# More sevenfold weight pairs in the down projection of a hybrid decoder layer, with more of their sums made ahead

## The chip, the cores and the metric

The kernel runs on one core of a Trainium2 chip. The metric is the device time of one execution in microseconds, the median of several. Less is better. The core has five engines with queues of their own: TensorE (PE; its weight loads are listed as PEld), VectorE (DVE), ScalarE (ACT), GpSimd (POOL) and SyncE (SP). SP, ACT and POOL also issue DMA transfers.

## The reference

One decoder layer over 256 tokens of width 2048, in float32. It is cut here to the order of its products; the change touches the last line alone, and the place of some vector work beside the others.

```python
h = rmsnorm(x, norm_mix_pre)
xr, yr, q, k, v, g_rnn, g_attn = split(h @ w_in)
y_rnn = rg_lru(conv(xr)) * gelu(yr)
y_att = sliding_window_sink_attention(rope(q), rope(k), v)
mix = sigmoid(g_rnn) * (y_rnn @ w_rnn_proj) + sigmoid(g_attn) * (y_att @ w_attn_proj)
x = x + rmsnorm(mix @ w_out, norm_mix_post)
u = square(relu(rmsnorm(x, norm_mlp_pre) @ w_mlp_up))      # 2048 -> 8192
return x + rmsnorm(u @ w_mlp_down, norm_mlp_post)          # 8192 -> 2048
```

## The kernel before

**Products in three parts.** Every float32 matrix is split into a high part (a cast, `Stream.two`, L176, on ACT) and a low part (source minus high, `Stream.low`, L181, on DVE). A product of two matrices is three matmuls: high by high, high by low, low by high (`product`, L1255). Weights stream through the class `Stream` in chunks of 128 x 2048 numbers (1 MB), each cut into items of 128 x 1024: a load on SP's queue into a raw slot, a cast on ACT into a `whi` slot, a subtraction on DVE into a `wlo` slot, then matmuls on PE. There are 4 raw slots and 6 high and low slots (L37), plus slots that a stage adds where it has room (`Stream.add`). `half` hands out one item of a plain chunk; before each, `ahead` emits the splits and loads of as many later items as there are slots.

**Stages.** Attention and gates projections, the recurrent branch, the attention and recurrent projections, the merge, the output projection (`o_pass`), and then the MLP in two halves `f` = 0, 1 of 4096 inner channels. A half has an up stage (16 calls of `a_pair` or `up_pair`, one per pair `p` of 256 inner channels, each 4 items) and two down passes `n` = 0, 1 (`down`, L1268 ff.), one per half of the output columns. A down pass works through the same 16 pairs.

**Plain and sevenfold pairs.** A plain pair in a down pass is 2 items by 4 output quarters: 8 products, 24 matmuls of 128 x 512. A sevenfold pair (`Stream.seven`, `LEFT`) forms sums of quarters of the weights (T1 to T4) and of the activations, as in Strassen's scheme in Winograd's form, and needs 7 products, 21 matmuls. It has 3 items of 128 x 1024 and one more piece of 128 x 512 (`t2`), which has 2 raw, 2 high and 2 low slots of its own. The products of a sevenfold pair go to seven PSUM banks: P1 and P6 in one `pair` tile, Q5 and N7 in the other, and P2, Q3, Q4. The first two tiles have the tag that the up stage's `ps` also uses (two buffers). Plain pairs use P2, Q3, Q4 and Cs. The products of one sevenfold pair are sorted by the weight they need: P1, Q3, P2, Q4, N7, Q5, P6.

**Who makes the sums.** `KINDS[f][n]` (L41) has one letter per pair. "1" is plain. For "3" DVE makes all sums as the pair is split (L149 to L151: one addition of 1024 columns and two of 512). For "4" all were made long before and lie in DRAM, so the pair loads 1.75 MB. For "2" T1 and T2 lie in DRAM (1.25 MB are loaded) and one subtraction on DVE (L147, 1024 columns) gives the third item; it needs `t2`, loaded by L114, and the first item.

**Sums ahead.** `sums_ahead` (L405 ff.) is a generator: a 1 MB load into an `early` buffer on POOL's queue (L410), four steps later two or one additions of 512 columns on DVE, a step later two more, then a store of 1 MB (kind 4) or 0.5 MB (kind 2) on POOL's queue (L422). `in_turn(n, every, wait)` starts n of them, one every `every` steps, after `wait` steps; a step is one call of `half` or `seven`. The buffers come from the pool `big` (12 units of 8 KB a partition), which also holds activations.

**Order.** Loops are unrolled. The tile framework lists the instructions of each engine at compile time in an order of its own within the dependences, and puts in the waits; the splits of sevenfold pairs are tied to program order on DVE and ACT (`behind_latest`). Each engine then works through its list in order, DMA issues on SP too. A buffer that is used again is waited for: the load of `t2` of a pair waits for the last reader of the `t2` two sevenfold pairs back, which is its low part (L181, `t2lo`).

At the end of an up stage the last `ps` tile is read by a copy on ACT (L359) and an addition on DVE (L360).

Of the kernel before, what the change touches and what calls it, by code (L numbers as in the profile page):

```python
# [18 lines left out]
F32 = mybir.dt.float32  # L19
F32R = mybir.dt.float32r  # L20
# [5 lines left out]
P = 128  # L26
# [11 lines left out]

PAIRS = 16

KINDS = ("1243414242143211", "1243414242143211"), ("1243441243424111", "1243441243424111")  # L41
SEVENS = [[p for p in range(PAIRS) if k[0][p] != "1"] for k in KINDS]


# [197 lines left out]
def layer(tc, x, few, kx_first, kx_rest, pos_row, gains, w_q, w_xy, w_rg, w_g, w_rp, w_ap, w_out,  # L242
# [44 lines left out]
    def unit(name, dt=F32R):  # L287
        return big.tile([P, 4, 2, S], dt, tag="U8", name=name)

    def flat(t):  # L290
        return t.rearrange("p a b c -> p (a b c)")
# [3 lines left out]
    def units(name):  # L295
        return [unit(f"{name}{i}") for i in range(4)]
# [507 lines left out]


    m1 = []
    ws.side.append(in_turn(11, 4, 16))
    for g in range(NKV):
        m1.append(pa.tile([P, TB, 512], F32, tag="m1", bufs=4, name=f"m1{g}"))
        for tb, b in enumerate(b_pass512(hT, two_banks("g"), 1)):  # L810
# [131 lines left out]
    for m in range(4):  # L942
        recur(m)
        if m == 0:
            pump(99)
            ctx_ps.close()
            psg = ctx1.enter_context(tc.tile_pool(name="psg", bufs=2, space=bass.MemoryType.PSUM))
            pairs.append(ctx1.enter_context(tc.tile_pool(name="psa2", bufs=1, space=bass.MemoryType.PSUM)))
        if m < 2:
            ws.side.append(in_turn(2, 6))  # L950
            for i in range(2):
                attn_proj(2 * m + i)
        if m < 3:
            gates(m)
# [83 lines left out]

    r1 = []
    late = []  # L1040
    h2T = units("h2T")

    def square(tb, q, b):
# [224 lines left out]
    def down(f, n, uT, held, order, finish, early, between=lambda p: None, behind=lambda: None, closing=False):  # L1268
# [8 lines left out]
        def step(p, i, hi, lo, name, at=0, w=512, into=None):  # L1277
            tb, n2 = name
            b = into or PLACE[name]
            o = 0 if into else at  # L1280
            t = slice(tb * P, tb * P + P)
            c = slice(n2 * 512 + at, n2 * 512 + at + w)
            a = uT[p][:, i]
            product(banks[b][:, o : o + w], (a[:, 0, t], a[:, 1, t]), (hi[:, c], lo[:, c]), b in begun,
                    p == PAIRS - 1 and i == 1, w < 512 and not into)
            begun.add(b)

        ready = {}
        for p in range(PAIRS - held - closing):
            if p in SEVENS[f]:  # L1290
# [3 lines left out]
                for name in names:  # L1294
                    i, w = LEFT[name]
                    product(banks[name], left(uT[p], i), parts[w], name in begun,
                            p == SEVENS[f][-1] and (name in ("P1", "P6", "Q5", "N7") or closing and name == PLACE[order[-1]]))
                    begun.add(name)
                if p == SEVENS[f][-1]:
                    for name in ((1, 0), (0, 0), (1, 1), (0, 1)):  # L1300
# [46 lines left out]
    for f in range(2):  # L1347
        uT = {}
        rooms = []
        if f:  # L1350
            ws.side.append(in_turn(7, 7))
        full = []
        for p in range(PAIRS):
            u = u2("u")
            if f == 0 and p == 1:
                ws.side.append(in_turn(6, 6, 16))
            if f == 0 and p in (4, 6):
                not_before(nc.gpsimd.dma_start(h2T_away[p // 2 - 2], h2T[p // 2].bitcast(F32)))
            if f == 0 and p < 2:
# [4 lines left out]
            if f == 0 and p == R2_AT:  # L1364
                pump(99)
                ctx3.close()
                pc = ctx2.enter_context(tc.tile_pool(name="pc", bufs=1))
                ws.small = pc
                ws.t2_raws, ws.t2_highs, ws.t2_lows = [[Slot() for i in range(2)] for k in range(3)]
                ws.add(ws.raws, pc.tile([P, 1024], F32, name="xraw"))  # L1370
            if f == 1 or p >= R2_AT:
                for q, u in full:
                    if q % 2 == 0:
# [7 lines left out]
                    evacuate(f, q, u, uT[q])  # L1381
                full.clear()
        order = [(1, 1), (1, 0), (0, 0), (0, 1)]
        more = [flat(unit("more", dt)) for dt in (F32, F32R)]
        for slots, room in ((ws.raws, more[0]), (ws.raws, more[0]), (ws.highs, more[1]), (ws.lows, more[1])):
            at = len(ws.added) % 2
            ws.add(slots, room[:, at * 1024 : at * 1024 + 1024])
        if f == 0:
            for n in range(2):
                def finish(name, b, t, *part):  # L1390
# [170 lines left out]
```

## Time and profile before

| | us |
|---|---|
| median of 3 runs | 1484.26 |
| lowest, highest | 1483.44, 1484.67 |
| the profiled execution | 1485.31 |
| its span, first to last instruction | 1483.5 |
| PE busy | 1473.4 |
| DVE busy | 1163.0 |
| ACT busy | 878.4 |

All times inside the kernel are from the profiled execution, from its span's start. Matmuls are pipelined, so a matmul's own duration is longer than its share of PE's time: what one costs is the distance from its start to that of the next. The same holds for DVE, where an instruction may begin a little before the one ahead of it has ended.

### The profile page before, as it was taken

How to read it: one execution, taken by the hardware profiler on the slowest of the kernel's cores; microseconds unless marked ns; L12 is line 12 of the kernel's file. 1: busy time of each engine (PE TensorE's matmuls, PEld its weight loads, DVE VectorE, ACT ScalarE, POOL GpSimd, SP SyncE). 2: the span in 40 equal slices, each digit the busy share in tenths (PEclk: the TensorE clock that was granted, in tenths of full speed). 3: DMA queues.
4: the chain of work that ended last, by engine and by line, in shares of the span. 5: the costliest groups of instructions: out<-in, count | busy, mean ns of one | idle time of the engine just before them, and what ended most of it. 6: DMA issues, size and time to landing. Idle time of an engine off the chain costs nothing.

```text
span 1483.5 us, 20572 instructions
## 1 busy us (share of the span) xinstructions
PE 1473.4 (99%) x7532; PEld 1250.5 (84%) x7532; DVE 1163.0 (78%) x1509; ACT 878.4 (59%) x1246; POOL 41.3 (3%) x83
## 2 busy tenths in 40 slices
PE   9999999999999999999999999999999999999997
PEld 8887788888889888888889888888888888888886
DVE  6687888869679967666757868788897777789997
ACT  8564565647566766444345756576565555666573
POOL 0000000000000000000000000000000000000000
PEclk9999999999999999999999999999999999999999
DMA  9778875585856567987764898888898778679795
GB/s 340 234 248 329 293 281 178 195 289 170 279 184 220 171 199 256 322 328 266 288 203 140 294 335 289 284 271 297 281 338 321 279 276 289 233 237 334 263 321 206
DMA packets 109830, 391.68 MB, mean 264 GB/s; under 512 B 12192, under 2 KB 12448, under 8 KB 101024
## 3 DMA queue, kind: packets, MB, share of 16 engines
q1 hardware_dynamic: 96192, 314.85, 61.5%
q0 software_dynamic: 10656, 70.26, 13.2%
q10 hardware_dynamic: 2880, 5.24, 0.9%
q8 instruction: 59, 0.97, 0.3%
q14 instruction: 43, 0.35, 0.1%
HBM read 351.51 MB, written 38.80 MB: 263 GB/s over the span
## 4 chain that ended last, share of the span: by engine, by line
PE 95%; DVE 3%; DMA 1%; ACT 1%; issue 0%; DVEq 0%; ACTq 0%
PE ps L332 22%; PE ps L330 11%; PE s L1255 8%; PE dQ L1255 8%; PE pp L372 4%; PE pp L370 4%; PE pp L374 4%; PE dP L1255 4%; PE g L370 4%; PE g L374 4%; PE g L372 4%; PE dCs L1255 2%; PE o L370 2%; PE o L372 2%; PE o L374 2%; PE q L370 2%
## 5 line engine op out<-in xcount | busy, mean ns | idle before, releaser
L181 DVE TENSOR_TENSOR wlo<-wraw,whi 128x1024 fp32r<-128x1024 f32 x444 | 539.0, 1221 | 209.0 <-ACT whi L176 204.7
L176 ACT CAST whi<-wraw 128x1024 fp32r<-128x1024 f32 x440 | 459.8, 1051 | 387.3 <-PE ps L332 89.7
L332 PE MATMUL ps<-h2T,whi 128*128 128x512 f32 x704 | 170.8, 391 | 0.3 <-DVE st L487 0.3
L332 PEld LDWEIGHTS ps<-h2T,whi 128*128 128x128 f32 x704 | 130.3, 188 | 26.2 <-DVE st L487 0.5
L332 PE MATMUL ps<-hT,whi 128*128 128x512 f32 x512 | 120.6, 391 | 0.0
L332 PEld LDWEIGHTS ps<-hT,whi 128*128 128x128 f32 x512 | 94.8, 188 | 19.4 <-issue 0.7
L370 PE MATMUL g<-whi,hT 128*128 128x512 f32 x256 | 100.9, 394 | 0.0
L372 PE MATMUL g<-wlo,hT 128*128 128x512 f32 x256 | 99.9, 390 | 0.0
L374 PE MATMUL g<-whi,hT 128*128 128x512 f32 x256 | 99.8, 390 | 0.0
L330 PE MATMUL ps<-h2T,wlo 128*128 128x256 f32 x704 | 91.8, 283 | 0.0
L330 PEld LDWEIGHTS ps<-h2T,wlo 128*128 128x128 f32 x704 | 89.6, 192 | 2.3
L1255 PE MATMUL dQ<-whi,uT 128*128 128x512 f32 (+1 forms) x210 | 78.2, 384 | 0.0
L176 ACT CAST whi<-more 128x1024 fp32r<-128x1024 f32 x48 | 50.2, 1053 | 35.3 <-DMA acc_away<-t 8.0
L181 DVE TENSOR_TENSOR wlo<-more,whi 128x1024 fp32r<-128x1024 f32 x48 | 58.1, 1222 | 10.8 <-ACT whi L176 9.6
L330 PEld LDWEIGHTS ps<-hT,wlo 128*128 128x128 f32 x512 | 63.7, 192 | 2.1 <-issue 0.8
L330 PE MATMUL ps<-hT,wlo 128*128 128x256 f32 x512 | 64.7, 284 | 0.0
L181 DVE TENSOR_TENSOR wlo<-xraw,whi 128x1024 fp32r<-128x1024 f32 x47 | 57.4, 1221 | 8.7 <-ACT whi L176 8.4
L176 ACT CAST whi<-xraw 128x1024 fp32r<-128x1024 f32 x47 | 49.2, 1048 | 20.2 <-PE ps L332 13.7
L370 PEld LDWEIGHTS g<-whi,hT 128*128 128x128 f32 x256 | 48.1, 188 | 10.5 <-issue 1.0
L1255 PE MATMUL s<-whi,uT 128*128 128x512 f32 (+1 forms) x166 | 56.5, 383 | 0.0
L374 PEld LDWEIGHTS g<-whi,hT 128*128 128x128 f32 x256 | 48.1, 188 | 10.0
L372 PEld LDWEIGHTS g<-wlo,hT 128*128 128x128 f32 x256 | 48.1, 188 | 9.5
(345 smaller groups left out, 2992.3 us busy)
## 6 DMA issues: line engine op xcount, KB each, us to landing
wraw<-in_w_up SPq DMA_DIRECT2D x103, 512.0 KB, 5.3
early<-in_w_dn POOLq DMA_DIRECT2D x36, 1024.0 KB, 8.4
wraw<-in_w_g SPq DMA_DIRECT2D x64, 512.0 KB, 5.2
wraw<-in_w_xy SPq DMA_DIRECT2D x64, 512.0 KB, 4.0
wraw<-in_w_dn SPq DMA_DIRECT2D x55, 512.0 KB, 5.9
away<-early POOLq DMA_DIRECT2D x22, 1024.0 KB, 6.6
wraw<-in_w_q SPq DMA_DIRECT2D x32, 512.0 KB, 5.4
wraw<-in_w_ap SPq DMA_DIRECT2D x32, 512.0 KB, 4.5
```

The lines of the kernel that those rows point to most:

```text
L176: self.pin(self.nc.scalar.copy(hi, src))
L181: self.latest_low = self.pin(self.nc.vector.tensor_tensor(lo, src, hi.bitcast(F32), ALU.subtract))
L330: mm(ps[:, f, 1, :], w, a[:, 0, :], start=False, stop=j == 1 and k == 7)
L332: mm(ps[:, f].rearrange("p a b -> p (a b)"), w, a.rearrange("p a b -> p (a b)"), start=kt == 0, stop=j == 3 and k == 7)
L370: mm(banks[tb][n], a[:, 0, t], hi[:, n * 512 : n * 512 + 512], start=first, stop=False)
L372: mm(banks[tb][n], a[:, 0, t], lo[:, n * 512 : n * 512 + 512], start=False, stop=False)
L374: mm(banks[tb][n], a[:, 1, t], hi[:, n * 512 : n * 512 + 512], start=False, stop=last)
L1255: mm(b, a[x], w[y], start=not begun and i == 0, stop=tail and i == 2, skip_group_check=shared)
```

## The change

14 instead of 11 pairs of each pass of the first half are sevenfold, and 12 instead of 11 in the second; the letters are dealt anew, so that kind "3" occurs 2 times instead of 8, "2" 24 instead of 14 and "4" 26 instead of 22. The sums made ahead rise from 36 chunks to 50: 13 instead of 11 in the attention stage (starting after 10 steps instead of 16), 3 instead of 2 in each attention projection, 8 as before in the merge, 4 new ones in the output projection, 9 every 4 steps instead of 6 every 6 in the first up stage, and 10 every 5 instead of 7 every 7 in the second. The first pair of every down pass, plain before, is sevenfold. There are now 14 `three` buffers instead of 11; for that the raw slot `xraw` is gone, and the second half's down passes get two raw slots more from a third `more` unit. So raw slots are 4 instead of 5 in the up stages, 6 instead of 7 in the first half's down passes, and 8 instead of 7 in the second's. The remaining lines set a matmul's `stop` flag where the last product now is.

```diff
--- before.py
+++ after.py
@@ -38,7 +38,7 @@
 
 PAIRS = 16
 
-KINDS = ("1243414242143211", "1243414242143211"), ("1243441243424111", "1243441243424111")
+KINDS = ("4242424242424211", "4242242242242411"), ("4242434242421111", "4242434242441111")
 SEVENS = [[p for p in range(PAIRS) if k[0][p] != "1"] for k in KINDS]
 
 
@@ -804,7 +804,7 @@
 
 
     m1 = []
-    ws.side.append(in_turn(11, 4, 16))
+    ws.side.append(in_turn(13, 4, 10))
     for g in range(NKV):
         m1.append(pa.tile([P, TB, 512], F32, tag="m1", bufs=4, name=f"m1{g}"))
         for tb, b in enumerate(b_pass512(hT, two_banks("g"), 1)):
@@ -947,7 +947,7 @@
             psg = ctx1.enter_context(tc.tile_pool(name="psg", bufs=2, space=bass.MemoryType.PSUM))
             pairs.append(ctx1.enter_context(tc.tile_pool(name="psa2", bufs=1, space=bass.MemoryType.PSUM)))
         if m < 2:
-            ws.side.append(in_turn(2, 6))
+            ws.side.append(in_turn(3, 7))
             for i in range(2):
                 attn_proj(2 * m + i)
         if m < 3:
@@ -1038,6 +1038,7 @@
 
     r1 = []
     late = []
+    ws.side.append(in_turn(4, 6, 2))
     h2T = units("h2T")
 
     def square(tb, q, b):
@@ -1282,7 +1283,8 @@
             c = slice(n2 * 512 + at, n2 * 512 + at + w)
             a = uT[p][:, i]
             product(banks[b][:, o : o + w], (a[:, 0, t], a[:, 1, t]), (hi[:, c], lo[:, c]), b in begun,
-                    p == PAIRS - 1 and i == 1, w < 512 and not into)
+                    (p == PAIRS - 1 or closing and p == PAIRS - held - 2 and name == order[-1]) and i == 1,
+                    w < 512 and not into)
             begun.add(b)
 
         ready = {}
@@ -1294,7 +1296,8 @@
                 for name in names:
                     i, w = LEFT[name]
                     product(banks[name], left(uT[p], i), parts[w], name in begun,
-                            p == SEVENS[f][-1] and (name in ("P1", "P6", "Q5", "N7") or closing and name == PLACE[order[-1]]))
+                            p == SEVENS[f][-1] and name in ("P1", "P6", "Q5", "N7")
+                            or closing and p == PAIRS - held - 2 and name == PLACE[order[-1]])
                     begun.add(name)
                 if p == SEVENS[f][-1]:
                     for name in ((1, 0), (0, 0), (1, 1), (0, 1)):
@@ -1348,12 +1351,12 @@
         uT = {}
         rooms = []
         if f:
-            ws.side.append(in_turn(7, 7))
+            ws.side.append(in_turn(10, 5))
         full = []
         for p in range(PAIRS):
             u = u2("u")
             if f == 0 and p == 1:
-                ws.side.append(in_turn(6, 6, 16))
+                ws.side.append(in_turn(9, 4, 8))
             if f == 0 and p in (4, 6):
                 not_before(nc.gpsimd.dma_start(h2T_away[p // 2 - 2], h2T[p // 2].bitcast(F32)))
             if f == 0 and p < 2:
@@ -1366,8 +1369,7 @@
                 ctx3.close()
                 pc = ctx2.enter_context(tc.tile_pool(name="pc", bufs=1))
                 ws.small = pc
-                ws.t2_raws, ws.t2_highs, ws.t2_lows = [[Slot() for i in range(2)] for k in range(3)]
-                ws.add(ws.raws, pc.tile([P, 1024], F32, name="xraw"))
+                ws.t2_raws, ws.t2_highs, ws.t2_lows = [[Slot() for i in range(n)] for n in (2, 2, 2)]
             if f == 1 or p >= R2_AT:
                 for q, u in full:
                     if q % 2 == 0:
@@ -1381,10 +1383,9 @@
                     evacuate(f, q, u, uT[q])
                 full.clear()
         order = [(1, 1), (1, 0), (0, 0), (0, 1)]
-        more = [flat(unit("more", dt)) for dt in (F32, F32R)]
-        for slots, room in ((ws.raws, more[0]), (ws.raws, more[0]), (ws.highs, more[1]), (ws.lows, more[1])):
-            at = len(ws.added) % 2
-            ws.add(slots, room[:, at * 1024 : at * 1024 + 1024])
+        more = [flat(unit("more", dt)) for dt in (F32, F32R) + f * (F32,)]
+        for i, slots in enumerate((ws.raws, ws.raws, ws.highs, ws.lows) + f * (ws.raws, ws.raws)):
+            ws.add(slots, more[i // 2][:, i % 2 * 1024 : i % 2 * 1024 + 1024])
         if f == 0:
             for n in range(2):
                 def finish(name, b, t, *part):
```

## Rows read from the trace of the kernel before

**Rows 1.** The page, part 1: the span, and busy time of each engine.

```profile
span 1483.5 us, 20572 instructions
PE 1473.4 (99%) x7532; PEld 1250.5 (84%) x7532; DVE 1163.0 (78%) x1509; ACT 878.4 (59%) x1246; POOL 41.3 (3%) x83
```

**Rows 2.** The chain that ended last, in order of time: start, us, instructions; first half's first down pass.

```profile
1016.60 2.72 PE s L1255 x12
```

**Rows 3.** Stretches: us, busy time (instructions) of five engines, clock, DMA share, GB/s.

```profile
842.41:975.77 133.36, 133.36 (x770) 118.16 (x769) 101.98 (x135) 80.13 (x107) 7.50 (x14) 1.00 0.83 293
979.04:1058.60 79.56, 79.56 (x353) 65.92 (x351) 71.08 (x73) 51.38 (x58) 0.00 (x0) 1.00 0.86 292
1058.60:1138.20 79.60, 79.60 (x353) 65.96 (x352) 70.89 (x72) 50.19 (x56) 0.00 (x0) 1.00 0.90 320
1315.97:1395.50 79.53, 79.53 (x352) 65.93 (x351) 73.57 (x78) 52.57 (x64) 0.00 (x0) 1.00 0.90 313
...
1125.00:1132.00 7.00, 7.00 (x32) 5.82 (x31) 6.39 (x8) 2.72 (x4) 0.00 (x0) 1.00 1.02 392
```

**Rows 4.** DVE in order of time (start, us, line, operation), last down pass.

```profile
1410.32 1.22 DVE L181 TENSOR_TENSOR more<-wraw,more 128x1024 fp32r<-128x1024 f32 x1
...
1413.72 0.69 DVE L181 TENSOR_TENSOR t2lo<-t,t2hi 128x512 fp32r<-128x512 f32 x1
1414.32 1.22 DVE L181 TENSOR_TENSOR wlo<-xraw,whi 128x1024 fp32r<-128x1024 f32 x1
...
1437.01 0.68 DVE L181 TENSOR_TENSOR t2lo<-t,t2hi 128x512 fp32r<-128x512 f32 x1
...
1441.62 1.22 DVE L147 TENSOR_TENSOR wraw<-t,more 128x1024 f32<-128x1024 f32 x1
...
1446.16 0.68 DVE L181 TENSOR_TENSOR t2lo<-t,t2hi 128x512 fp32r<-128x512 f32 x1
1446.76 1.22 DVE L181 TENSOR_TENSOR wlo<-wraw,whi 128x1024 fp32r<-128x1024 f32 x1
```

**Rows 5.** DVE in order of time, the first half's first down pass.

```profile
1008.71 0.69 DVE L181 TENSOR_TENSOR t2lo<-t,t2hi 128x512 fp32r<-128x512 f32 x1
...
1015.23 1.22 DVE L147 TENSOR_TENSOR wraw<-t,more 128x1024 f32<-128x1024 f32 x1
```

**Rows 6.** SP's DMA issues in order of time: two loads of `t2`.

```profile
1009.42 0.33 SPq L114 DMA_DIRECT2D t<-away  x1
...
1437.72 0.32 SPq L114 DMA_DIRECT2D t<-away  x1
```

**Rows 7.** Line L114 over the span, all loads of `t2` of kind 2.

```profile
L114 SPq DMA_DIRECT2D t<-away x14: 320/326/425, 837.2 to 1437.7; - x14
...
DMA to landing us min/median/max: 3.0/5.2/7.0
```

**Rows 8.** Line L119 over the span: the first item's loads of sevenfold pairs.

```profile
DMA to landing us min/median/max: 3.3/6.3/8.3
```

**Rows 9.** All engines in order of time, where each up stage ends (PE, then DVE).

```profile
979.04 0.39 PE L1255 MATMUL dQ<-whi,uT 128*128 128x512 f32 x1
...
981.39 0.69 DVE L360 TENSOR_TENSOR u<-ps,u 128x512 f32<-128x512 f32 x1
...
1315.97 0.39 PE L1255 MATMUL dQ<-whi,uT 128*128 128x512 f32 x1
...
1318.33 0.69 DVE L360 TENSOR_TENSOR u<-ps,u 128x512 f32<-128x512 f32 x1
```

**Rows 10.** The page, parts 2 and 6: GB/s by fortieths; DMA issues, KB, us to landing.

```profile
GB/s 340 234 248 329 293 281 178 195 289 170 279 184 220 171 199 256 322 328 266 288 203 140 294 335 289 284 271 297 281 338 321 279 276 289 233 237 334 263 321 206
...
wraw<-in_w_up SPq DMA_DIRECT2D x103, 512.0 KB, 5.3
early<-in_w_dn POOLq DMA_DIRECT2D x36, 1024.0 KB, 8.4
...
away<-early POOLq DMA_DIRECT2D x22, 1024.0 KB, 6.6
```

## The prediction

> **What bounds the kernel now.** I read the page first. PE is busy for 1473.4 of 1483.5 us, DVE for 1163.0, ACT for 878.4 [rows 1]. A busy PE need not be PE at its rate, so the next view is the chain that ended last: inside a down pass it is PE alone, 12 matmuls of 128 x 512 in 2.72 us [rows 2], 0.2267 us each. A plain pair (24) then costs 5.44 us, a sevenfold one (21) 4.76. A pass of 11 sevenfold and 5 plain pairs should take 11 x 4.76 + 5 x 5.44 = 79.56 us. The table by stretches has the passes at 79.56, 79.60 and 79.53, with the clock at 1.00 throughout [rows 3]. So PE never waits there, and the passes are bound by the count of matmuls. The same table shows what is near: DVE is busy for 71.1, 70.9 and 73.6 us of these passes, and the DMA engines for 0.86 to 0.90 of them. The reader is to see a kernel with one bound and two others close under it: a saving on PE counts in full only as far as DVE and DMA keep up.
>
> **What the change removes.** 3 + 3 pairs in the first half's passes and 1 + 1 in the second's turn sevenfold: 8 pairs, 8 x 3 = 24 matmuls, 24 x 0.2267 = 5.44 us. All lie on PE's unbroken chain, so all count, if nothing new makes PE wait. The passes would go to 77.52 us (first half) and 78.88 (second).
>
> **What it puts on DVE.** A low part begins 1.13 us after the one before it and a `t2lo` takes 0.60: a kind 4 pair goes from start to the next start in 1410.32 to 1414.32, 4.00 us; a kind 2 pair, with its subtraction, in 1441.62 to 1446.76, 5.14 us [rows 4]. PE gives a sevenfold pair 4.76. Kinds 4 and 2 in turn average 4.57, so DVE keeps up on average, at 96%; the first pass has seven of each, 64.0 us against 66.6 for PE. In the second pass eight are kind 2: 65.1 against 66.6. The plain pairs, which let DVE catch up (4 low parts would be 2.27 us of 5.44 for each), are gone from the middle of these passes. The dearer kind 3 is nearly gone too, which is why the sum holds. Activations of the 8 extra pairs and the 14 extra chunks summed ahead cost DVE some 1 to 2.4 us each (two to four additions or casts' low parts of 0.60) in stages where it is busy for 102 of 133 us [rows 3]; I cost them at nothing there, since a low part that is late by one such group is covered by six `whi` slots, each worth more than 2.7 us of PE.
>
> **The wait that decides: `t2`.** A kind 2 pair begins on DVE with a subtraction that needs its `t2`, and that load waits for the `t2lo` two sevenfold pairs back (two slots). With a kind 4 pair between, DVE has 4.00 us of work to cover the load. Two cases in the trace show it. After the `t2lo` that ended at 1437.69 the load went out at 1437.72 and the subtraction began at 1441.62, with no idle time, 3.93 us later [rows 4, 6]. After the one that ended at 1009.40 the load went out at 1009.42 and the subtraction began at 1015.23, 5.83 us later, 1.8 more than the pair between takes [rows 5, 6]. All 14 such loads took 3.0 to 7.0 us, median 5.2 [rows 7]. With L for that latency and 0.1 us for the release, two pairs (4, 2) cost DVE 5.14 + L + 0.1 as soon as L exceeds 3.9, and PE 9.52: they keep pace up to L = 4.3. Above it DVE falls back by L - 4.3 every two pairs and eats its lead.
>
> The first pass worked through, from its start: I take pair 1's `t2lo` done at 2.6 us (the slots full as now, one more low part, `t2lo` and the addition L360), pair 2 at 7.8 with one more activation, pair 3 at 12.95. Pairs 5, 7, 9, 11, 13 follow at 5.24 + L each. PE needs pair 13's first item at 13 x 4.76 = 61.88; it is there 2.87 us (two low parts and `t2lo`) before that pair's end. At L = 5.0 this is 12.95 + 51.2 - 2.87 = 61.3, in time by 0.6. At L = 5.6 it is 64.3, and PE stands for 2.4 us. In the second pass the letters go 4, 2, 2, so there is one wait in three pairs, and the same count gives 0 at 5.0 and 1.7 at 5.6. The second half gives 0 and 0.4, and for the last pass, with its extra scalings on DVE, 0.5 and 1.8. I take L = 5.0, the middle of 3.0 to 7.0 and a little under the median: 0.5 us in all. The ends are 0 (L up to 4.4) and, at L = 7.0 throughout, over 20 us; that nobody sees for six loads in a row here.
>
> **The raw slots.** With six in the first half's passes, a pair's first load goes out when the first low part two pairs back is done; from 9.52 us some 2.3 go for its own low part and cast, which leaves 7.2 us. These loads took 6.3 us in the median and 8.3 at most [rows 8]. Nothing at the median, 1 us now and then at the worst; it acts in the same direction as a long L and belongs to that rival.
>
> **A cover that goes.** The first pair of a pass is now sevenfold. In the first pass of each half its fifth product, N7, goes to the pair tile that the up stage's last `ps` occupied, and that is read by L360. PE's first matmul is at 979.04, L360 ends at 982.08; in the second half 1315.97 and 1319.02 [rows 9]. Before, a plain pair that uses other banks hid this for 5.44 us. Now N7 is wanted 4 x 0.68 = 2.72 us after the start, and is free after 3.04 to 3.05: 0.33 us and a release, say 0.4, twice: 0.8 us. If L360 is listed one low part later it is 1.5 each, if earlier nothing.
>
> **Sums ahead, and DMA.** Extra loads and stores ride on POOL's queue, on which nothing else waits but the two stores of h2T. Most new ones lie in stages with room: the output projection, and the earliest steps of attention (fortieths of 140 to 250 GB/s near them, [rows 10]). The tight place is the first up stage, one sum per pair instead of one per 1.5. A pair there takes 133.36 / 12 = 11.11 us [rows 3] and loads 4 x 0.524 MB, 189 GB/s; a sum reads 1.05 MB and writes 1.05 or 0.52 (five of nine are kind 4), 168 GB/s; the stores of h2T, 2.1 MB over some 100 us, 21. Together 377 GB/s, against 293 at a DMA share of 0.83 now. While loads were bunched the engines moved 392 GB/s at a share of 1.02 [rows 3]. So it fits, without room to spare, and I cost it at nothing: cover is the lead of six items. The Trainium skill speaks against it: DMA: Bandwidth & Descriptors, Specifications, gives one core about 358 GB/s of HBM. By that the 100 us would take 5 us longer and the change would come out at 1484 or 1485, no change. The row of 392 is above that figure; it is 7 us, not 100.
>
> **Sum.** -5.44 + 0.8 + 0.5 = -4.1 us. The profiled execution took 1485.31, 1.05 above the median of 1484.26, which is in the spread of the runs; I set the sum against the median: **1480.1 us**. Against the profiled execution itself it would be 1481.2.
>
> **Rivals.** (1) The `t2` chain runs out of lead. With the DMA engines fuller L goes to 5.6: stalls of 2.4 + 1.7 + 0.4 + 1.8 = 6.3 us, so 1484.26 - 5.44 + 0.8 + 6.3 = 1485.9. For it: the median of 5.2 is already over 4.3, and the first half's passes will move more (1.75 and 1.25 MB a pair in turn, one raw slot less). Against it: the last pass had 3.93 us without a wait, and a DVE that is behind issues its loads later, into emptier queues. (2) Slower: the first up stage is bound by DMA. By proportion of the share, 293 / 0.83 = 353 GB/s is the limit, and no fortieth of the span held over 341 [rows 10]. At 341, 100 us of 377 GB/s take 10.6 us longer; when the six items of lead are spent PE waits in the up stage or enters the pass without lead: 1484.26 - 4.64 + 10.6 = 1490.2. Below about 352 GB/s sustained the change ends over 0.2% slower. Against: 392 in the bunched stretch. (3) The passes don't lose 24 matmuls, or the saved time was hidden: the even 0.2267 us and the sums of 79.56 speak against, 2 in 100.
>
> **How the numbers follow.** Forecast 0.50; rival 1 0.30; rival 2 0.18; rival 3 0.02. A measurement of this kernel tells some 0.2%, 3.0 us, from no change. Faster by more (under 1481.3) is the forecast, 0.50. Within it lie rival 1, except its worst, and rival 3: 0.31. Slower (over 1487.2) takes rival 2 and the worst of rival 1: 0.19. The low end is the full 5.44 us with no stall, 1478.8, less 0.3 of spread; the high end goes to 1489, most of the way into rival 2.
>
> **What would show it.** Right: 7508 matmuls; first-half passes of 77.5 and second-half ones of 78.9 us; a PE gap of 0.3 to 0.5 us ahead of N7 at each first pass; subtractions on L147 that wait for `t2` on DMA in nearly every kind 2 pair without PE waiting. Rival 1: gaps on PE ahead of a product with `whi`, `wlo` or `t2lo`, growing late in the passes. Rival 2: pairs of the first up stage longer than 11.11 us, with low parts waiting for casts and casts for loads, at 340 to 355 GB/s. Wrong altogether: stalls in the attention or projection stages, where new `early` buffers could push out others of the 12.

## The result and the profile after

The changed kernel is slower. It takes 1496.63 us (median of 5, 1489.85 to 1499.53), the kernel before beside it 1484.67 (1483.44 to 1485.38): ratio 1.0077, 95% interval 1.0064 to 1.0090. 1480.1 was predicted, and the measured time lies above every one that the prediction gave, its worst rival (1490.2) included. Its executions lie further apart than those of before, over some 10 us, and the profiled one was the fastest: 1489.85 us, span 1488.0. A second profile, of the same kernel in the first experiment, took 1498.65. Both are needed to see the loss.

The page, part 1, answers [rows 1]: 24 matmuls are gone, and PE's busy time fell by 0.8 us, where 5.44 were due.

```profile
span 1488.0 us, 20759 instructions
PE 1472.6 (99%) x7508; PEld 1243.7 (84%) x7508; DVE 1199.6 (81%) x1579; ACT 890.3 (60%) x1266; POOL 56.3 (4%) x111
```

The table of stretches answers [rows 3]: us, busy time (instructions) of PE, its weight loads, DVE, ACT and POOL, clock, DMA share, GB/s. The rows are twelve pairs of the first up stage and the first half's two down passes.

```profile
844.10:977.50 133.40, 133.40 (x770) 118.15 (x769) 109.02 (x153) 82.04 (x110) 10.13 (x19) 1.00 0.90 335
980.75:1058.66 77.91, 77.83 (x344) 64.11 (x342) 72.85 (x74) 54.08 (x64) 0.00 (x0) 1.00 0.92 318
1058.66:1140.93 82.27, 79.70 (x343) 63.57 (x342) 75.27 (x77) 55.02 (x62) 0.00 (x0) 1.00 0.93 325
```

The up stage is as long as before (133.36), with DMA at 335 GB/s. The first pass takes 77.91 us, 0.4 over the 77.52 of its matmuls; the second takes 82.27, 4.75 over, longer than the 79.60 it took with three sevenfold pairs less. (In the second profile they lose 2.3 and 5.8.) So the wait that PE never had in a down pass is there now.

Set beside before, matmul by matmul, the time goes as follows (us; in brackets the stall above the matmuls' own time, 155.0 for the first half's two passes, and 158.1 for the second's with the 0.34 of smaller matmuls at the very end):

| | before | after | after, second profile |
|---|---|---|---|
| lost up to the first down pass | 0 | 1.7 | 5.5 |
| first half's two passes | 159.1 | 160.2 (5.1) | 163.1 (8.1) |
| second half's two passes | 159.5 | 161.2 (3.1) | 163.3 (5.2) |

The first line is the start of the first down pass against the one in the profile of before; other kernels here, with no gap at the gates, came there up to 1.7 us sooner, so it is good to a microsecond or two. In it 1.7 us in both profiles fall to the gates, near 480 us; the second profile loses 3.8 more ahead of and in the output projection. That makes three places. The experiments take them in turn.

### The profile page after: what moved, and what is told of

It is laid out like the page before. It is cut to its first block, busy times and chain, and to the rows that moved or that the text cites. A ratio compares the mean times of both kernels' runs of the same rounds, so it can differ in the third digit from the quotient of the medians.

```text
span 1488.0 us, 20759 instructions
## 1 busy us (share of the span) xinstructions
PE 1472.6 (99%) x7508; PEld 1243.7 (84%) x7508; DVE 1199.6 (81%) x1579; ACT 890.3 (60%) x1266; POOL 56.3 (4%) x111
## 3 DMA queue, kind: packets, MB, share of 16 engines
q10 hardware_dynamic: 2880, 5.24, 0.9%
## 4 chain that ended last, share of the span: by engine, by line
PE 75%; DVE 10%; DMA 9%; ACT 3%; issue 3%; SPq 0%; DVEq 0%; ACTq 0%
PE ps L332 19%; PE ps L330 10%; DVE wlo L181 5%; PE pp L374 4%; PE pp L372 4%; PE pp L370 4%; PE g L370 4%; PE g L374 4%; PE g L372 4%; DMA more<-in_w_dn 3%; PE dQ L1256 3%; PE s L1256 2%; PE q L370 2%; PE q L374 2%; PE q L372 2%
## 5 line engine op out<-in xcount | busy, mean ns | idle before, releaser
L176 ACT CAST whi<-wraw 128x1024 fp32r<-128x1024 f32 x481 | 502.0, 1050 | 427.7 <-PE pp L374 71.1
L181 DVE TENSOR_TENSOR wlo<-wraw,whi 128x1024 fp32r<-128x1024 f32 x485 | 587.1, 1222 | 167.8 <-ACT whi L176 166.5
L372 PE MATMUL g<-wlo,hT 128*128 128x512 f32 x256 | 99.7, 389 | 0.0
L176 ACT CAST whi<-more 128x1024 fp32r<-128x1024 f32 x61 | 63.4, 1050 | 28.4 <-DMA more<-in_w_dn 12.7
L181 DVE TENSOR_TENSOR wlo<-more,whi 128x1024 fp32r<-128x1024 f32 x61 | 73.4, 1221 | 2.8 <-ACT whi L176 2.0
L1256 PE MATMUL s<-whi,uT 128*128 128x512 f32 (+1 forms) x190 | 64.8, 384 | 0.0
L1256 PE MATMUL dQ<-whi,uT 128*128 128x512 f32 (+1 forms) x172 | 62.5, 384 | 0.0
L370 PEld LDWEIGHTS g<-whi,hT 128*128 128x128 f32 x256 | 48.1, 188 | 10.5 <-issue 1.0
L410 POOL DMA_DIRECT2D early<-in_w_dn x50 | 26.8, 536 | 793.4 <-DVE wlo L181 500.8
L372 PEld LDWEIGHTS g<-wlo,hT 128*128 128x128 f32 x256 | 48.1, 188 | 9.5
L414 DVE TENSOR_TENSOR early<-early 128x512 f32<-128x512 f32 x50 | 34.4, 688 | 25.5 <-DMA early<-in_w_dn 25.2
```

What stands on the lines that cost most here:

```text
L176: self.pin(self.nc.scalar.copy(hi, src))
L181: self.latest_low = self.pin(self.nc.vector.tensor_tensor(lo, src, hi.bitcast(F32), ALU.subtract))
L370: mm(banks[tb][n], a[:, 0, t], hi[:, n * 512 : n * 512 + 512], start=first, stop=False)
L372: mm(banks[tb][n], a[:, 0, t], lo[:, n * 512 : n * 512 + 512], start=False, stop=False)
L410: not_before(nc.gpsimd.dma_start(w, chunks[c]))
L414: v.tensor_tensor(t1, t1, t3, ALU.add)
```

## Experiments: the parts that cost little, and the sums ahead

**The change again, unedited.** 

> The changed kernel once more, unedited, for a profile of another execution: the one on hand took 1489.85 us and four others 1496.0 to 1499.5, so some 7 us of the loss are in no trace yet. Theory A, the loops of slots in the down passes (a load waits for the split that frees its slot, the split for the load): all of the extra time lies in the four down passes, which took 160.2 us for the first half's two and 161.0 for the second's and would be 5 to 10 us longer together, and the up stages stay at 11.11 us a pair. Theory B, the DMA engines are overfull in the first up stage (339 GB/s there): that stage, 146.8 us from 833.0 on, is 3 to 8 us longer instead. Theory C, early buffers that keep others out: the extra time is before 800 us, around the gates, where this trace already loses 1.7 us.

1495.32 us, ratio 1.0064 (1.0044 to 1.0084). The loss repeats; the third column of the table is its profile.

**The raw slots alone**: before, with the slots of after.

```diff
-                ws.add(ws.raws, pc.tile([P, 1024], F32, name="xraw"))
...
+        more = [flat(unit("more", dt)) for dt in (F32, F32R) + f * (F32,)]
...
```

> The kernel before with one part of the change, the raw slots: no xraw, two more in the second half's down passes; letters and sums ahead as before. Theory A in its form for the raw slots: passes with plain pairs between have time to spare, so little is lost, 1484 to 1487 us, but loads wait for slots more often in the first half's passes. Theory B: no change in what is moved, 1484.3. If four raw slots in the up stages are what hurts, a pair there is over 11.11 us and the time 1487 to 1495.

1485.18 us, 1.0003 (0.9994 to 1.0013): no change that the times can tell. The profile does show one: PE waits once, at 992 us, for a low part, and the first half's passes take 160.5 us where before they took 159.1. So with the letters of before six raw slots cost some 1.3 us there, in this one profile.

**The output projection's sums alone**, added to before.

```diff
+    ws.side.append(in_turn(4, 6, 2))
```

> The kernel before with four of its 36 sums ahead moved into the output projection (one every 6 steps from step 2 on), everything else as before. Theory D, which the second profile of the changed kernel suggests: loads and stores of these sums meet the 4 MB that SP loads for the residual and the gains there, weight loads come late and PE waits; 0 to 4 us, different from run to run: median 1485 to 1488, spread of 3 us or more, and no PE gap at the gates near 480 us. Theory A (only the down passes lose): 1484.5 with the spread of before.

1484.79 us, 1.0004 (0.9995 to 1.0013): no change.

**All sums ahead, with the letters of before.** The edits in the five stages are those of the change (two of them shown):

```diff
-    ws.side.append(in_turn(11, 4, 16))
+    ws.side.append(in_turn(13, 4, 10))
-            ws.side.append(in_turn(2, 6))
+            ws.side.append(in_turn(3, 7))
```

> The kernel before with the new numbers of sums ahead (13 from step 10 on, 3 and 3, 8, 4, then the remaining 5 every 4 steps in the first up stage, none in the second), letters and raw slots as before; 36 sums in all. Theory C: the loss of 1.7 us at the gates is there, 1486, and nothing else. Theory B in its mild form (crowded transfers in the attention to output projection stages): 1487 to 1490. Theory A: nothing in the passes, which stay at 79.6 us each; 1484.3 to 1486.

1488.47 us, 1.0026 (1.0017 to 1.0035), with not one matmul less. Its profile is of its fastest execution (1485.43); there the passes are as before, and 1.2 us are lost at the gates. So some sums cost time that the prediction put at nothing.

**The third sum in the attention projections alone.**

```diff
-            ws.side.append(in_turn(2, 6))
+            ws.side.append(in_turn(3, 7))
```

> The kernel before with one edit: three sums ahead, one every seven steps, in each attention projection in place of two every six. If the third sum costs the time at the gates: PE gaps of 1.2 to 1.8 us near 478 to 482 us as in the changed kernel, 1485.4 to 1486.1. If it takes the other edits too (13 sums earlier, starting sooner): no gap, 1484.3.

1486.53 us, 1.0017 (1.0007 to 1.0026): 2.0 us for this edit by itself. The rest of the 3.9 us that all sums cost together is not divided up. The profile of this run has the gap at the gates, 1.1 us, and one of 2.1 near 649, where loads of `in_w_g` and `in_w_rp` took 10 to 11 us. How the gap at the gates comes about, the changed kernel's timeline shows (start, us, engine, line, operation; in brackets the idle time before it and what ended it):

```profile
479.14 0.19 PEld L894 LDWEIGHTS pg<-xs,whi 128*128 128x128 f32 x1 [0.89 <-ACT room L899]
...
481.44 0.19 PEld L894 LDWEIGHTS pg<-xs,whi 128*128 128x128 f32 x1 [0.84 <-ACT room L899]
```

PE waits for ACT to empty one of the two `pg` banks. ACT is late because it casts in order and its casts had waited for weights. ACT's waits from 440 to 476 us, before and then after (total, times, longest):

```profile
ACT whi L176 <- DMA wraw<-in_w_xy: 3.6, 6, 1.1
```

```profile
ACT whi L176 <- DMA wraw<-in_w_xy: 10.7, 6, 3.8
```

The loads are hardly slower (median landing 4.5 against 4.3 us), and DMA is far from full there (217 GB/s from 440 to 460, against 203 before). They go out later, and the delay begins on DVE. The third sum is loaded at 420.06, and its additions (L419, L420) stand in DVE's list ahead of a low part that frees a raw slot. DVE in order of time, before and then after:

```profile
441.91 1.22 DVE L181 TENSOR_TENSOR wlo<-wraw,whi 128x1024 fp32r<-128x1024 f32 x1
```

```profile
442.02 0.69 DVE L419 TENSOR_TENSOR early<-early 128x512 f32<-128x512 f32 x1
...
444.41 0.67 DVE L420 TENSOR_TENSOR early<-early 128x512 f32<-128x512 f32 x1
...
445.59 1.22 DVE L181 TENSOR_TENSOR wlo<-wraw,whi 128x1024 fp32r<-128x1024 f32 x1
```

Operations of the recurrent branch (L922, L923, L927) that stood behind this low part before now stand ahead of it too, so it comes 3.7 us later, and SP issues the load that waits for its slot at 446.88 instead of 443.15. The run with the third sum alone has the same order (L419 at 441.37, the low part at 444.94). So what is lost is the lead of the stream, not bandwidth: PE still has data, but ACT does the gates' work (L899) 1.3 to 1.9 us later, behind casts that wait.

**The changed kernel with two sums in each attention projection**, the rest of it kept (the two left over go to the second up stage).

```diff
-            ws.side.append(in_turn(3, 7))
+            ws.side.append(in_turn(2, 6))
-            ws.side.append(in_turn(10, 5))
+            ws.side.append(in_turn(12, 4))
```

> The changed kernel with one thing undone: two sums in each attention projection instead of three (the two left over go to the second up stage, 12 every four steps). All 24 matmuls stay saved. If the third sum costs what it cost alone (2.0 us) and nothing else depends on it: 1493. If it also brings the gaps in the output projection: no gap at the gates, 0.2 us in the output projection, and 1490 to 1492, with the stalls of the down passes (8 to 13 us over both halves) unchanged.

1491.21 us, 1.0046 (1.0030 to 1.0061): 4 to 5 us better than the change. The profile has no gap at the gates and loses 1.0 us in the output projection. The second up stage, which has more sums here than in the change, loses 0.9, and the down passes 7.2 and 3.2. So the third sum costs more with the other edits than alone; the gaps of 3.8 us in the second profile of the change (PE ahead of L372, for low parts on DVE, after casts that waited 14.7 us in all for loads of `in_w_out`) were not seen without it. That they hang on it is an inference from one profile each.

## Experiments: the down passes

**The change in the first half only**: second half's letters, attention projections and output projection as before; the sums left over go to the second up stage.

```diff
-KINDS = (...), ("4242434242421111", "4242434242441111")
+KINDS = (...), ("1243441243424111", "1243441243424111")
```

> The changed kernel with the second half's letters as before (11 pairs), 2 instead of 3 sums in each attention projection, none in the output projection, and 12 every 4 steps in the second up stage. It saves 4 x 3 x ... 18 matmuls, 4.1 us. Theory A: the first half's two passes lose 5 to 8 us as in the changed kernel, the second's (8 raw slots, plain pairs between) lose 0 to 1: 1486 to 1489, with a spread of 2 us. Theories C and D: the gaps at the gates and in the output projection are gone, so the difference to the changed kernel, 6 to 9 us, is more than the passes give.

1488.83 us, 1.0034 (1.0023 to 1.0044). The first half's passes take 163.7 us, 8.7 over; the second half's are as before, and there is no gap at the gates or in the output projection. So these stalls need neither the third attention sum nor the output projection's. (The sums in the first up stage are as in the change.)

The chain of waits of the changed kernel in the first pass has a loop that closes every two pairs (start, us, what):

```profile
1005.13 0.70 DVE t2lo L181
1005.84 0.32 SPq L114
1006.16 0.05 issue
1006.22 0.42 SPq L121
1006.64 0.05 issue
1006.69 4.45 DMA more<-in_w_dn
1011.20 0.04 issue
1011.24 1.06 ACT whi L176
1012.33 1.50 DVE wlo L181 x2
1013.83 0.78 issue
1014.61 0.70 DVE t2lo L181
```

The `t2lo` frees a slot; SP, which had stood at the `t2` load (L114), issues it; then the loads of the pair's second item (L121, L122) go out, whose raw slots were free by then; ACT casts, DVE subtracts, and the next `t2lo` ends the loop. From `t2lo` to `t2lo` that is 9.48 us here and 9.7 and 10.1 in the next two turns, against PE's 9.52. The wait for a slot is not only `t2`'s: it holds SP's queue. DVE's waits from 985 to 1130 us (total, times, longest) say the same: it stands mostly for casts, and at the subtraction (L147) for `t2` just once. (Before, casts cost it 7.6 us there too, but plain pairs came between and let it catch up.)

```profile
DVE wlo L181 <- ACT whi L176: 8.7, 10, 2.3
DVE more L147 <- DMA t<-away: 1.2, 1, 1.2
```

**`t2` loaded on POOL's queue**, so that SP is not held:

```diff
-                self.latest = load(self.t2[c], away[:, 0:512])
+                self.nc.gpsimd.dma_start(self.t2[c], away[:, 0:512])
```

> The changed kernel with one line other: the loads of t2 of kind 2 go out on POOL's queue instead of SP's, so that the loads of the second item are no longer queued on SP behind a t2 load that waits for its slot. Theory A2 (the loop of t2lo, the waiting t2 load, the second item's load behind it on SP, its cast and three low parts, 0.8 + 5.8 + 1.1 + 3.0 = 10.7 us for two pairs where PE needs 9.5): the down passes lose 4 to 8 us less, 1488 to 1491 in the median, and SP issues L121 before the t2 load. Theory A1 (the t2 latency itself, or the six raw slots, is the loop): within 2 us of 1495.

1517.84 us, 1.0239 (1.0212 to 1.0266). The `t2` loads now take 5.1/5.9/8.1 us (least, median, most) and 0.54 to issue, against 2.9/3.8/6.6 and 0.32 on SP in the first half's passes. DVE in order of time in the first pass:

```profile
1018.38 0.68 DVE L181 TENSOR_TENSOR t2lo<-t,t2hi 128x512 fp32r<-128x512 f32 x1
...
1022.39 0.68 DVE L181 TENSOR_TENSOR t2lo<-t,t2hi 128x512 fp32r<-128x512 f32 x1
1024.86 1.23 DVE L147 TENSOR_TENSOR wraw<-t,more 128x1024 f32<-128x1024 f32 x1 [1.79 <-issue]
```

The subtraction begins 5.80 us after the end of the `t2lo` two pairs back, and from its start to the end of its own `t2lo` it is 5.24: a loop of 11.04 us; PE's gaps in this pass came every 10.9 to 11.0. This is the loop of the prediction, with a longer L: with SP's queue free, the subtraction is what waits. The 1488 to 1491 expected of theory A2 was missed by far.

**`t2` loaded behind the second item**, on SP. 

> The changed kernel with the t2 load of kind 2 written behind the second item's loads instead of ahead of the first item's, still on SP. Theory A2: the second item no longer waits for the t2 slot; the loop is t2lo, the t2 load alone (3.8 us in the median) and 5.2 us of DVE, 9.4 us for two pairs, so the passes keep PE's pace: 4 to 8 us less than the changed kernel, 1488 to 1491. Theory A1: no change, 1494 to 1497. If the raw slots are the loop it is no change either, and ACT waits for DMA of the first item.

1496.68 us, 1.0087 (1.0072 to 1.0102): no better; A2 had said 1488 to 1491 here too. The second item is no longer held, but `t2` goes out later, and what stands behind it now is the next pair. SP's waits from 985 to 1130 us show it still stopped for a `t2` slot, 29 us in all:

```profile
SPq L125 <- DVE t2lo L181: 19.6, 9, 4.7
...
SPq L122 <- DVE t2lo L181: 9.7, 13, 0.9
```

(In that kernel the lines are shifted; L122 is `t2` of kind 2, L125 that of kind 4.) So the order on SP is not the cause by itself. What is left is the number of slots: of `t2`, or of raw slots.

**12 pairs**, then the 6 KB that they leave free given to `t2` or to a raw slot. Three kernels, the first the base:

```diff
-KINDS = ("4242424242424211", "4242242242242411"), ...
+KINDS = ("4242424242421111", "4242242242241111"), ...
```

> The change in the first half only, but with 12 sevenfold pairs a pass (letters 4242424242421111 and 4242242242241111) where the run with 14 had them; second half as before. Two raw slots of t2, six raw slots. This is the base for the two runs that follow, which use the 6 KB a partition that two `three` buffers less leave free. Without stalls the two first-half passes take 2 x 78.88 = 157.8 us, against 159.2 before: 1482.9. Both theories (A: the loop through the two raw slots of t2; B: six raw slots are too few) expect stalls that begin where the lead is spent, some 2 to 6 us, fewer than with 14 pairs since four plain pairs at the end need nothing of either: 1485 to 1489.

> The run with 12 pairs, with four raw slots of t2 in place of two; raw slots stay six. A (the loop through the t2 slots): the load of t2 no longer waits for the t2lo two pairs back but for the one four back, so the stalls of the first half's passes go to under 0.5 us: 1482.5 to 1483.5. B (raw slots): stalls stay as in the run with 12 pairs, within 1 us.

> The run with 12 pairs, with the raw slot xraw given back (seven raw slots in the first half's passes), t2 slots two as before. A: stalls stay within 1 us of the run with 12 pairs. B: they go to under 0.5 us, 1482.5 to 1483.5.

1484.3, 1483.04 and 1483.04 us (1.0001, 0.9993 and 0.9993; intervals of some 0.2%). The stalls are 1.2, 0.0 and 0.0 us. With four plain pairs at the end so little is lost that either remedy covers it: this set doesn't tell the two theories apart. With the seventh raw slot SP still stood for a slot of `t2` from 985 to 1130 us, about as long as in the base (19.0 us), and PE lost nothing:

```profile
SPq L114 <- DVE t2lo L181: 19.8, 10, 4.3
```

So that wait is not a cost by itself. That it becomes one where too few loads have gone out ahead of it is our reading.

**14 pairs with four slots of `t2`, and five raw slots**, since there was no other room. 

> The change in the first half only, all 14 pairs, with one raw slot of the `more` unit cut into two raw slots for t2: four of t2, five raw slots (six in the second half). A: the stalls of 8.7 us in the first half's passes (163.7 us against 155.0 without any) fall below 2: 155 to 157 us for both passes, and 1480 to 1483 in all. B: with five raw slots they grow, to 12 or more: 1491 and over. Falling by half would mean that both act.

1491.26 us, 1.0048 (1.0033 to 1.0063); the passes take 165.5, 10.5 over. From `t2lo` to `t2lo` a kind 2 pair takes 5.14 us nearly everywhere (up to 5.57), where the changed kernel has up to 6.4; but a kind 4 pair, 4.01 in most places there, takes up to 6.17. SP waits for `t2` for 4.2 us between 985 and 1130, and for raw slots (L119, L121, L124) for 16.7 to 22.4 at each line. Five raw slots are too few for 14 pairs. The theory of `t2` had said 1480 to 1483 for this run and missed, since the remedy took away what the stage had just enough of.

**13 pairs, two against three slots of `t2`**, six raw slots in both. One edit between them:

```diff
-                ws.t2_raws, ws.t2_highs, ws.t2_lows = [[Slot() for i in range(n)] for n in (2, 2, 2)]
+                ws.t2_raws, ws.t2_highs, ws.t2_lows = [[Slot() for i in range(n)] for n in (3, 2, 2)]
```

> The change in the first half only, with 13 sevenfold pairs a pass (4242424242424111, 4242242242242111), two raw slots of t2, six raw slots; second half as before, the third attention sum and the output projection's sums left out. Ideal for the two first-half passes: 2 x 78.20 = 156.4 us against 159.2. With 12 pairs 1.2 us were lost to stalls and with 14 pairs 8.7; if the two slots of t2 set the pace of the kind 2 pairs, 13 lose something between, 3 to 5: 1484.5 to 1486.5.

> The run with 13 pairs, with three raw slots of t2 in place of two (the 3 KB a partition of one `three` buffer less make room); raw slots stay six. If the loop of t2 sets the pace: t2lo to t2lo of kind 2 pairs goes to 5.14 us in most places, stalls under 0.7 us, 1481.5 to 1482.5. If the raw slots set it: as the run with 13 pairs, within 0.8 us, with the kind 4 pairs longer than 4.01 us, as they were with five raw slots.

1484.64 us (1.0003, 0.9993 to 1.0012) and 1482.21 us (0.9986, 0.9977 to 0.9996). With 13 pairs and six raw slots a third slot of `t2` is enough, so the raw slots alone do not set the pace. That the slots of `t2` alone do is not shown: 13 or 14 pairs with two slots of `t2` and a seventh raw slot, the other remedy at 12, were not run. The stall with two slots was 2.3 us, less than the 3 to 5 expected. SP's waits for a `t2` slot from 985 to 1130 us (total, times, longest), first in before, then in the changed kernel, then with 13 pairs and two slots, and with 13 and three:

```profile
SPq L114 <- DVE t2lo L181: 12.4, 7, 4.3
```

```profile
SPq L114 <- DVE t2lo L181: 28.0, 12, 3.4
```

```profile
SPq L114 <- DVE t2lo L181: 26.8, 11, 4.0
```

```profile
SPq L114 <- DVE t2lo L181: 2.4, 6, 0.8
```

The two passes as stretches, each over its own time (two slots, then three; columns as above):

```profile
978.10:1136.70 158.60, 157.58 (x691) 129.16 (x690) 143.30 (x145) 105.83 (x121) 0.00 (x0) 1.00 0.92 320
```

```profile
978.40:1134.80 156.40, 156.40 (x691) 129.50 (x691) 142.62 (x145) 106.53 (x121) 0.00 (x0) 1.00 0.94 328
```

With three slots the passes take 156.40 us, which is the matmuls alone (2 x 78.20). And the loads of `t2` take longer: 3.9/6.3/7.5 us against 3.1/4.2/7.2. Latency went up by half and the stall went away, because SP no longer stands at that load, and what is queued behind it goes out. One pair of the two-slot run: SP's issues, where the first item's load (L119) goes out right behind the `t2` load that had waited, and DVE, where the subtraction waits for that load, 7 us on:

```profile
1080.18 0.32 SPq L114 DMA_DIRECT2D t<-away  x1
1080.56 0.52 SPq L119 DMA_DIRECT2D wraw<-in_w_dn  x1
```

```profile
1085.48 0.68 DVE L181 TENSOR_TENSOR t2lo<-t,t2hi 128x512 fp32r<-128x512 f32 x1
1087.66 1.23 DVE L147 TENSOR_TENSOR wraw<-t,wraw 128x1024 f32<-128x1024 f32 x1 [1.49 <-DMA wraw<-in_w_dn]
```

**A candidate with both remedies**: 13 pairs and three `t2` slots in the first half, two attention sums, and the second half of the change.

```diff
-KINDS = ("4242424242424211", "4242242242242411"), ...
+KINDS = ("4242424242424111", "4242242242242111"), ...
-            ws.side.append(in_turn(3, 7))
+            ws.side.append(in_turn(2, 6))
-[[Slot() for i in range(n)] for n in (2, 2, 2)]
+[[Slot() for i in range(n)] for n in (3, 2, 2)]
```

> A candidate: the change with 13 pairs in the first half's passes in place of 14, three raw slots of t2, and without the third sum in each attention projection; 12 pairs in the second half, its eight raw slots and the four sums in the output projection as in the change. If the t2 loop and the third attention sum are what cost the change its gain: no gap at the gates, 0.2 us in the output projection, first-half passes 156.4 to 157.2, second-half ones 157.8 to 158.5: 1480.2 to 1481.5. If the rest of the loss was from DMA load by the extra sums in the up stages, stalls of several us stay and it ends over 1484.

1485.23 us, 1.0007 (0.9998 to 1.0016). No gap at the gates, none in the output projection, first-half passes 156.5: with both remedies, and one pair less a pass, both losses are gone. But the second half, which was expected at 157.8, loses 3.9 us in its up stage and 4.2 in its passes. In the up stage the chain shows a load of `in_w_up` that takes 9.17 us, on four raw slots:

```profile
1272.27 9.17 DMA wraw<-in_w_up
```

Soon after it PE stands 1.6 us for a low part near 1285. At the end of the stage DVE comes late to L360, and PE waits 1.0 us for it ahead of the product that takes over the `ps` tile; that the long load is what made it late is not shown. In the last pass DVE takes the kind 2 pairs at 5.14 us without a wait for `t2`, and PE stands for 2 us near 1465, after a load of 10.14 us (plain items there take 9.4/9.8/10.7) and 14 us in which DVE has no idle time: it makes low parts and the first sums of the results (L1307 to L1310, L1418) in turn. The three slots of `t2` hold in the second half too, and its passes still lose 4.2 us, between the 3.1 and 5.2 of the change with two. So a third slot of `t2` did not help there. Long loads on four raw slots, and a DVE without slack at the end, are what the trace suggests. Neither was tried by itself, and the second half's loss stays open.

**The kernel with 13 pairs and three slots, once more.** 

> The run with 13 pairs in the first half's passes and three raw slots of t2, unedited, in more rounds: the best kernel so far. It measured 2.3 us under before, where 4 pairs x 3 matmuls x 0.2267 = 2.72 were taken out. If that holds: 1481.5 to 1482.5, ratio 0.998 to 0.999.

1481.76 us, 0.9984 (0.9975 to 0.9993): 2.6 us faster than before, where its 12 matmuls make 2.72. It is the best kernel here.

## Why the prediction was wrong, point by point

- **What bounds the kernel, and the price of a matmul**: right. 24 matmuls fewer; with three `t2` slots the passes come out at 78.20 us each to the hundredth.
- **DVE's cost of a pair**: right. From `t2lo` to `t2lo` kind 4 takes 4.01 us and kind 2 5.14 wherever nothing waits.
- **The wait for `t2`**: this is the step that failed most. The prediction had the slot and the `t2lo` that frees it right, but not the path between them: it said 0.5 us, and the down passes lost 8.2 and 13.3 in the two profiles of the change, 5.1 and 8.1 of them in the first half, which this loop concerns (what the second half lost stays open). It took the load's latency as all that the slot costs, and the DVE subtraction as what waits. What the runs show is SP's queue held behind the load that waits: L121, L122 and the next pair's L119 go out late, and DVE stands at a low part for a late cast (8.7 us against 1.2 at L147 for `t2`, where waits in nearly every kind 2 pair were forecast). L was even below the assumed 5.0 (3.8 in the median), and rival 1's condition, a usual L of 5.6, never came; the stalls that rival 1 gave as its sign, late in the passes, came without it. The cause is shown with 13 pairs, where the stall was 2.3 us; that the larger one with 14 is the same is inferred from the same waits, since no run took it away with 14.
- **How the rows for it were read**: the second of the two cases, 5.83 us from `t2lo` to subtraction, was taken as DVE waiting for the load. No idle time stands ahead of that subtraction, and its load had landed (5.6 us); 1.3 of the 1.8 us went in waits for casts inside the pair between:

```profile
1010.29 2.59 DVE L181 TENSOR_TENSOR wlo<-wraw,whi 128x1024 fp32r<-128x1024 f32 x2 [0.89 <-ACT whi L176]
...
1014.62 0.69 DVE L181 TENSOR_TENSOR t2lo<-t,t2hi 128x512 fp32r<-128x512 f32 x1 [0.38 <-ACT t2hi L176]
```

  In the whole of before DVE stood at L147 for `t2` once, for 0.3 us, behind the load that took 7.0. The waits for casts were in the trace, and so was SP's wait for `t2lo`, 12.4 us in this stretch; what stood behind it was not asked.
- **The lead at the start of the second pass**: the first pass was taken over for the second. In the first, pair 1's `t2lo` ended 3.0 us after the start (2.6 said), and the pass lost 0.4; in the second it ended 5.5 after, as DVE has four additions of the first pass's results (L1394, 0.60 each) between, and the pass lost 4.75. So 2.5 us of lead were spent before the loop began.
- **Sums ahead at nothing**: wrong for the attention projections, 2.0 us alone and 4 to 5 among the other edits. The step weighed DVE's time against PE's cover by the `whi` slots. It left out that a late low part also keeps its raw slot: the next load went out 3.7 us later, ACT's cast waited for it, and the gates' work stood behind that cast. The last sentence of the prediction had named these stages as the place of an error, but by another way (buffers pushed out), which no row shows. For the output projection's sums alone the term held.
- **Raw slots at nothing**: right for the edit alone as far as the times tell, though its profile loses 1.3 us. With more pairs the slot counts: at 12 a seventh took 1.2 us of stalls to none, and at 14 five were too few even with four slots of `t2`. Whether six are enough for 14 no run shows.
- **N7 and L360, 0.8 us**: none in the changed kernel's first profile; L360 was listed early enough (it ended 2.44 us after the start of the first pass, against 3.04). In the second half of other profiles it is there: 0.3 us in the second profile of the change, 1.0 in the candidate, 1.4 with two attention sums.
- **Rival 2, the first up stage bound by DMA**: no. 335 GB/s over 133 us cost PE nothing. The Trainium skill (DMA: Bandwidth & Descriptors, Specifications) gives some 358 GB/s for one core; by it the stage would have had no room for the 377 that the prediction asked of it, and the trace shows 335, so it was not put to the test there. In the candidate 20 us of a down pass ran at more, which is above that figure:

```profile
1360.00:1380.00 20.00, 20.00 (x90) 16.57 (x89) 20.00 (x20) 15.68 (x18) 0.00 (x0) 1.00 1.03 406
```

## What to carry to other kernels

A load that waits for its buffer on an in-order queue delays every load behind it, so a small buffer with few slots can set the pace of a large stream: ask the queue's own waits, and what stands behind the instruction that waits, before pricing the wait by that load's latency. When an engine is at 96% of the bound, a wait that used to be recovered in a slack stretch is paid for; the slack was the plain pairs, and with four, three and two of them at the end of a pass the stalls were 1.2, 2.3 and 8.7 us. Work that is moved beside a stream can stand in an engine's list ahead of what frees the stream's buffers; then it costs more than its own time, and the price appears later, at the first tight hand-over between engines.

## What was not expected of the hardware

The same 256 KB load, in two kernels that differ in its line alone, took 5.9 us in the median on POOL's queue and 3.8 on SP's, and 0.54 against 0.32 us to issue. Single loads of 512 KB took 9.17, 10.14 and 11.40 us in the experiments, where the median of the weights' loads over the page of the changed kernel is 6.3 (`in_w_up`). And a longer latency (6.3 against 4.2 us) went with a faster pass.
